# Weight halves by casting and accumulating loads, in place of a load, a cast and a subtraction

## The chip, the core and the metric

The kernel runs on one core of one Trainium2 chip. A core has five engines that run side by side and wait for each other by semaphores: TensorE (PE, matrix products; its weight loads are shown as PEld), VectorE (DVE), ScalarE (ACT), GpSimd (POOL) and SyncE (SP, which here only issues transfers). Transfers between the device memory and the on-chip memory run on 16 DMA engines; SyncE or GpSimd issue them. The metric is the time of one execution on the device, in microseconds, as the median of several runs.

## The reference, cut to what matters

One layer of a hybrid encoder is computed for 512 prompt tokens and 32 tokens of a running stream, 544 columns together: an input projection, three token mixers in parallel (RG-LRU, Mamba-2 SSD and HGRN2), their merge by gates, an output projection, and a SwiGLU FFN.

```python
h = rmsnorm(x, p['norm_mix'])
proj = h @ p['w_in']
z, xbc, dt_raw, hq, hf, hi, hgate, rgate, rx, mg = jnp.split(proj, split_pts, axis=-1)
...
pb = jnp.einsum('kblc,kcd->kbld', branches, p['w_branch'])
gates = jax.nn.sigmoid(mg.reshape(b, L, N_BRANCH, D_MODEL))
merged = jnp.einsum('kbld,blkd->bld', pb, gates)
x = x + merged @ p['w_out']
h2 = rmsnorm(x, p['norm_ffn'])
g, u = jnp.split(h2 @ p['w_ffn_in'], [FF_HIDDEN], axis=-1)
x = x + (jax.nn.silu(g) * u) @ p['w_ffn_out']
```

All of `w_in`, `w_branch`, `w_out`, `w_ffn_in` and `w_ffn_out` is float32, some 100 MB, and is read once.

## The kernel before

The products need more precision than one pass gives, so each operand is split into two halves of the type fp32r: a high half (the value cast to fp32r) and a low half (the value minus the high half). For weights w and activations x, TensorE adds up wh·xh + wh·xl + wl·xh.

All weights are cut into 101 groups of 256 columns, called **keys** here (lines 65 to 88). A key holds 8 blocks of 128 rows (128 x 2048 float32 on chip, 1 MB), but for the four last keys of `w_ffn_out`, which hold 6. Each key serves two **steps**: a step is one tile of 128 output columns, with 8 blocks times three passes times two halves of the tokens = 48 matmuls of 128x272. Within a step the products (line 263) run wh against both halves of the activations first, 32 matmuls, then wl against the high half, 16 matmuls.

How the weights come: `load_raw` (line 241) has SyncE load a key's float32 into `raw`, a pool with two buffers. `prep` (line 248) makes the halves of one step: ScalarE casts 128x1024 into `wh` (line 258), VectorE subtracts it from `raw` into `wl` (line 259); both pools have three buffers of a step's size. `run_program` (line 284) goes through the list of steps, has the halves prepared one step ahead, and the keys loaded two keys ahead of the preparation. What each engine does in which order is settled when the program is built; each engine then runs its list in order.

Between the products stands the mixers' work, in three stages: the RG-LRU (to about 190 us), the SSD (to about 490 us) and the HGRN2 (585 to 856 us). It uses VectorE, ScalarE, GpSimd and small matmuls. After each step an evacuation reads the step's accumulator (two buffers) by ScalarE or VectorE. From 493 to 585 us and after 856 us (branch product, output projection, FFN) TensorE has products alone.

GpSimd in the program before issues no transfers; it fills and copies small tiles, raises to the power -0.5 for the norms (line 167 and line 1064), and in the HGRN2 copies the blocks `bd` into `at` (line 1013).

The head (line 443) is written by hand: SyncE loads x (eight tiles `xt`) and in between the first key, rx0, in four pieces; ScalarE and VectorE split x (`yr`) and rx0 block by block; three tiles of products start before the norm of x is known, two from rx0 and one from the second key, rg0. The norm's factor `rs_x` comes from a sum of squares `ssx` (line 465), a power on GpSimd (line 167), and is brought into the layout of the columns by transposes on TensorE (line 172).

Of the kernel before, what the change touches and what calls it, by code (L numbers as in the profile page):

```python
# [11 lines left out]
F = _mybir.dt.float32  # L12
R = _mybir.dt.float32r
# [5 lines left out]
P = 128  # L19
# [18 lines left out]
LEVELS = (16, 32, 64)  # L38
# pacing of the mixers' work between the products: DVE microseconds to a tile of products, by phase
PACE_RG, PACE_RG_END, PACE_SSD, PACE_HG = 3.0, 4.0, 5.5, 3.5  # L40
# [13 lines left out]

# columns of the packed parameters, by channel of a tile; the first NHALF are used halved
HALVED = (("ba", 8), ("bi", 8))
# [8 lines left out]
def weight_groups():  # L65
    """key -> its blocks (matrix, first row, rows, first column, columns), 256 columns together"""
    g = {}
    for i in range(4):
        g[f"rx{i}"] = [("w_in", 0, D, C_RX + 256 * i, 256)]
        g[f"rg{i}"] = [("w_in", 0, D, C_RG + 256 * i, 256)]  # L70
        g[f"bc{i}"] = [("w_in", 0, D, C_XBC + 1024 + P * i, P), ("w_in", 0, D, C_XBC + 1536 + P * i, P)]
        g[f"xb{i}"] = [("w_in", 0, D, C_XBC + 256 * i, 256)]
        g[f"z{i}"] = [("w_in", 0, D, C_Z + 256 * i, 256)]
        for nm, c in (("hf", C_HF), ("hq", C_HQ), ("hi", C_HI), ("hgt", C_HG)):
            g[f"{nm}{i}"] = [("w_in", 0, D, c + 256 * i, 256)]
        for b in range(3):
            g[f"mg{b}_{i}"] = [("w_in", 0, D, C_MG + D * b + 256 * i, 256)]
            g[f"br{b}_{i}"] = [(f"w_branch{b}", 0, D, 256 * i, 256)]
        g[f"wo{i}"] = [("w_out", 0, D, 256 * i, 256)]
        for kg, (k0, nk) in enumerate(KG):  # L80
            g[f"fo{i}_{kg}"] = [("w_ffn_out", k0 * P, nk * P, 256 * i, 256)]
    for m in range(NF):
        g[f"fi{m}"] = [("w_ffn_in", 0, D, P * m, P), ("w_ffn_in", 0, D, FF + P * m, P)]
    return g
# [16 lines left out]
def hybrid_layer(ctx: ExitStack, tc: _tile.TileContext, a: dict, outs: list):  # L101
# [27 lines left out]

    # ---------------------------------------------------------------- constants and parameters  # L130
    hhi = hpool.tile([P, NK, T], R, tag="hhi", name="hhi")
# [26 lines left out]
    def token_rstd(ssq, n, name):  # L158
        """1/sqrt(mean + eps) by token, from squares summed over the channel tiles"""
        p = mx()  # L160
# [13 lines left out]

    # ---------------------------------------------------------------- derived parameters
    hga1, hgna1, hgb1, rgc, rgnc = (ctile([P, 8], n) for n in ("hga1", "hgna1", "hgb1", "rgc", "rgnc"))
# [24 lines left out]
    def derived():  # L201
        # a softmax over the layers, minus its first row summed up: one layer, so each row is its own maximum
        lbv = ctile([P, 8], "lbv")
# [13 lines left out]

    # ---------------------------------------------------------------- the stream of matrix products
    sides = []
# [18 lines left out]

    RAWB = 2

    def load_raw(key):
        g, nk = WG[key]
        t = wpool.tile([P, NK, 256], F, tag="raw", name="raw", bufs=RAWB)
        nc.sync.dma_start(t[:, :nk, :], wp[g].rearrange("p (k n) -> p k n", n=256)[:, :nk, :])
        raws[key] = t


    def prep(st):
        if st.wh is not None:
            return  # L250
        if st.share:
            st.wh, st.wl = st.share.wh, st.share.wl
            return
        r = raws[st.raw]
        st.wh = wpool.tile([P, NK, P], R, tag="wh", name="wh")
        st.wl = wpool.tile([P, NK, P], R, tag="wl", name="wl")
        src = r[:, : st.nk, st.col : st.col + P]
        S.activation(st.wh[:, : st.nk, :], src, AF.Copy)  # L258
        V.tensor_tensor(st.wl[:, : st.nk, :], src, st.wh[:, : st.nk, :].bitcast(F), ALU.subtract)  # L259

# [23 lines left out]
    def run_program():  # L284
# [9 lines left out]
        for s in program:  # L294
# [3 lines left out]
            while prepped < min(len(order), done + 2):  # L298
                st = order[prepped]
                while loaded < min(len(keys), pos[st.raw] + RAWB):  # L300
                    if keys[loaded] not in raws:
                        load_raw(keys[loaded])
                    loaded += 1
                prep(st)
                prepped += 1
# [12 lines left out]

    # phase pools ------------------------------------------------------------
    st_yr = ExitStack()  # L320
# [56 lines left out]

    # ---------------------------------------------------------------- gates and branches
    gate_th = {}
# [33 lines left out]

    # ---------------------------------------------------------------- RG-LRU
    sd = {}
# [19 lines left out]

    # ---------------------------------------------------------------- head
    # the first tiles take x before its norm, and the norm's factor by token after the products
    hd = {}
# [4 lines left out]
    def head():  # L443
# [8 lines left out]
        load_raw("rg0")  # L452
        whs = [wpool.tile([P, NK, P], R, tag="wh", name="wh") for _ in range(2)]
        wls = [wpool.tile([P, NK, P], R, tag="wl", name="wl") for _ in range(2)]
        derived()
# [162 lines left out]

    # ---------------------------------------------------------------- SSD
    xb_cv, gz, y_mb = {}, {}, {}  # L620
# [67 lines left out]
    def ssd_side(g):  # L688
# [29 lines left out]
        yield 3.0  # L718
        # C B^T and token-major B
        p = mx()  # L720
# [24 lines left out]
        dt, eacs, etot, wend = (sd[k] for k in ("dt", "eacs", "etot", "wend"))  # L745
        # token-major x, times dt and times the decay to the chunk's end
        xdt = pt_([P, 4, 256], "xdt")
# [21 lines left out]
        yield 0.7  # L769
        # states  # L770
        Hh = pt_([P, 4, 256], "Hh")
# [22 lines left out]

        # outputs
        yint = pt_([P, 4, 256], "xw")
# [19 lines left out]
        yield 0.6  # L816
        # both parts by channel, skip, gate, norm
        p5 = mx()
# [63 lines left out]

    # ---------------------------------------------------------------- HGRN
    hv, y_hg = {}, {}
# [34 lines left out]
    def hg_side(h):  # L919
# [21 lines left out]
        bds = pt_([TS, 32], "bds", 2)  # L941
        # within 16 tokens by two levels of four parts each: in every block, the queries of the parts
        # after part 0, 1 and 2, decayed to the part's end, meet its keys, also decayed to the part's end
        qv = pt_([P, T // 4, 10], "qv", 1)
# [148 lines left out]

    # ---------------------------------------------------------------- merge out, residual
    x1 = {}
# [26 lines left out]

    # ---------------------------------------------------------------- FFN
    ff = {}
# [64 lines left out]
    def fin_evac(m, hs):  # L1189
        """the tokens of some halves: the residual, token-major, times the norm's weight, and its squares"""  # L1190
        def f(acc):
# [64 lines left out]
def lay_out(v):  # L1256
    """The arrays that the program takes, from those of setup_inputs: layout only."""
    cm = lambda x: x.reshape(-1, P).T
# [64 lines left out]
```

## Time and profile before

| what | us |
|---|---|
| median of 3 runs | 1379.65 (1379.39 to 1381.41) |
| span of the profiled execution, first to last instruction | 1377.6 |
| outside the span, by the median | 2.05 |
| TensorE busy | 1359.3 |
| VectorE, ScalarE, GpSimd busy | 725.0, 531.3, 101.5 |
| bytes moved | 115.37 MB, mean 84 GB/s |

The profile has one such page and answers to queries on the trace behind it. A row of a group reads: line of the kernel, engine, operation, output from inputs with partitions x elements and type, number of such instructions, then the busy time and the mean time of one in nanoseconds, then how long the engine sat idle ahead of them and what ended that. A row of the timeline starts with the time from the span's start and the duration in us. A row of the windows lists, for a stretch of time, the busy time of each engine with its number of instructions, the granted clock of TensorE, the share of the 16 DMA engines in use, and the GB/s. In a row of waits stand the waiting engine with its line, the engine and line waited for, and the us in total, the times and the longest.

### The profile page before, as it was taken

To read this page: it belongs to the slowest core of one execution; us is meant where nothing else is said; L and a number is where in the kernel's file an instruction comes from. 1 tells how busy PE (TensorE), PEld (TensorE's weight loads), DVE (VectorE), ACT (ScalarE), POOL (GpSimd) and SP (SyncE) were. 2 spreads that over 40 slices of the span, in tenths; PEclk is the share of its full clock that TensorE was granted. 3 is DMA by queue.
4 is the path that set the end of the run, shared out by engine and by line. 5 is a ranking of instruction groups with operands and counts; after the bars stand their busy time and mean duration, and the time that the engine had idled before them with its cause. 6 is when DMAs were issued, how large, how long until landed. Compare 5 with 4: busy or idle time off the path is not lost.

```text
span 1377.6 us, 26147 instructions
## 1 busy us (share of the span) xinstructions
PE 1359.3 (99%) x11374; PEld 1316.6 (96%) x11374; DVE 725.0 (53%) x1337; ACT 531.3 (39%) x884; POOL 101.5 (7%) x200
## 2 busy tenths in 40 slices
PE   7999999999999999999999999999999999999997
PEld 7999999899998999999999999999999999999996
DVE  7987654737575644374747464455443443332222
ACT  6785744235445321333343433234222222222222
POOL 2031001021020000011010101000000000000000
PEclk9999999999999999999999999999999999999998
DMA  6212122212121122221212121242222222222211
GB/s 232 93 62 93 62 96 87 79 62 70 66 72 66 70 82 83 85 68 68 70 67 88 49 85 47 92 157 93 73 81 93 92 92 92 88 83 87 87 73 65
DMA packets 23634, 115.37 MB, mean 84 GB/s; under 512 B 2624, under 2 KB 7616, under 8 KB 11488
## 3 DMA queue, kind: packets, MB, share of 16 engines
q1 hardware_dynamic: 23520, 113.70, 23.6%
q8 instruction: 89, 1.46, 0.4%
q14 instruction: 25, 0.20, 0.0%
HBM read 109.29 MB, written 4.41 MB: 83 GB/s over the span
## 4 chain that ended last, share of the span: by engine, by line
PE 96%; DVE 1%; ACT 1%; issue 1%; DMA 0%; POOL 0%; SPq 0%; POOLq 0%; DVEq 0%
PE acc L277 83%; PE mx L563 1%; PE mx L829 1%; PE mx L831 1%; PE mx L972 1%; PE mx L1036 1%; PE mx L1051 1%; PE mx L931 1%; PE mx L776 1%; PE mx L1018 0%; PE mx L162 0%; PE mx L705 0%; PE mx L1053 0%; DMA xt<-in_xT_dram 0%; PE mx L805 0%
## 5 line engine op out<-in xcount | busy, mean ns | idle before, releaser
L258 ACT ACTIVATE wh<-raw 128x1024 fp32r<-128x1024 f32 (+1 forms) x194 | 203.7, 1051 | 452.6 <-PE acc L277 435.7
L259 DVE TENSOR_TENSOR wl<-raw,wh 128x1024 fp32r<-128x1024 f32 (+1 forms) x194 | 234.7, 1210 | 195.8 <-PE acc L277 174.7
L277 PE MATMUL acc<-hhi,wh 128*128 128x272 f32 x1472 | 316.5, 294 | 0.0
L277 PE MATMUL acc<-hlo,wh 128*128 128x272 f32 x1472 | 306.6, 289 | 0.0
L277 PEld LDWEIGHTS acc<-hhi,wh 128*128 128x128 f32 x1472 | 232.1, 188 | 6.1 <-issue 1.5
L277 PEld LDWEIGHTS acc<-hlo,wh 128*128 128x128 f32 x1472 | 231.2, 188 | 0.5
L277 PE MATMUL acc<-hhi,wl 128*128 128x272 f32 x1472 | 206.7, 290 | 0.0
L277 PEld LDWEIGHTS acc<-hhi,wl 128*128 128x128 f32 x1472 | 191.8, 188 | 2.9 <-issue 1.3
L277 PE MATMUL acc<-x1lo,wh 128*128 128x272 f32 x704 | 146.1, 288 | 0.0
L277 PE MATMUL acc<-x1hi,wh 128*128 128x272 f32 x704 | 145.8, 288 | 0.0
L277 PEld LDWEIGHTS acc<-x1hi,wh 128*128 128x128 f32 x704 | 110.9, 188 | 0.0
L277 PEld LDWEIGHTS acc<-x1lo,wh 128*128 128x128 f32 x704 | 110.4, 188 | 0.0
L277 PE MATMUL acc<-yr,wh 128*128 128x272 f32 x800 | 106.9, 289 | 0.1
L277 PEld LDWEIGHTS acc<-yr,wh 128*128 128x128 f32 x800 | 102.5, 188 | 0.9 <-ACT yr L345 0.3
L277 PE MATMUL acc<-x1hi,wl 128*128 128x272 f32 x704 | 96.0, 288 | 0.0
L277 PEld LDWEIGHTS acc<-x1hi,wl 128*128 128x128 f32 x704 | 91.4, 188 | 0.0
L277 PE MATMUL acc<-fhi,wh 128*128 128x272 f32 x352 | 74.7, 289 | 0.0
L277 PE MATMUL acc<-flo,wh 128*128 128x272 f32 x352 | 74.5, 289 | 0.0
L1158 DVE TENSOR_TENSOR fg<-acc,rb 128x544 f32<-128x544 f32 x22 | 15.9, 725 | 76.5 <-PE acc L277 74.6
L1169 DVE TENSOR_TENSOR fg<-fg,acc 128x544 f32<-128x544 f32 x22 | 15.9, 721 | 76.1 <-PE acc L277 76.1
L277 PEld LDWEIGHTS acc<-fhi,wh 128*128 128x128 f32 x352 | 55.8, 189 | 0.1
L277 PEld LDWEIGHTS acc<-flo,wh 128*128 128x128 f32 x352 | 55.8, 188 | 0.0
(368 smaller groups left out, 1748.9 us busy)
## 6 DMA issues: line engine op xcount, KB each, us to landing
raw<-in_weights_dram SPq DMA_DIRECT2D x93, 1024.0 KB, 4.7
raw<-in_weights_dram SPq DMA_DIRECT2D x4, 768.0 KB, 4.1
xt<-in_xT_dram SPq DMA_DIRECT2D x8, 272.0 KB, 5.7
yr<-in_xT_dram SPq DMA_DIRECT2D x8, 272.0 KB, 5.7
out_dram<-otok SPq DMA_DIRECT2D x4, 512.0 KB, 3.2
raw<-in_weights_dram SPq DMA_DIRECT2D x4, 256.0 KB, 5.6
wab<-in_rg_gates_dram SPq DMA_DIRECT2D x1, 1024.0 KB, 4.6
h0s<-in_ssm_in_dram SPq DMA_DIRECT2D x4, 128.0 KB, 3.9
```

The costliest lines, as they stand in the source:

```text
L258: S.activation(st.wh[:, : st.nk, :], src, AF.Copy)
L259: V.tensor_tensor(st.wl[:, : st.nk, :], src, st.wh[:, : st.nk, :].bitcast(F), ALU.subtract)
L277: PE.matmul(acc[:, h, :HALF], l, r[:, h * HALF : (h + 1) * HALF], start=st.first and i == 0, stop=st.last and i == len(seq) - 1)
L563: PE.matmul(p[:, :WH], l[:, i, ct, :], r[:, s], start=n == 0, stop=n == 2)
L776: PE.matmul(p[:, i * 256 : (i + 1) * 256], btok[:, c, :], xw[:, c, :], start=True, stop=True)
L829: PE.matmul(p[64 * (r % 2) : 64 * (r % 2) + 64, s], xdt[:, c, r * 64 : (r + 1) * 64], lts[c][:, r, :], start=c == 0, stop=False)
L831: PE.matmul(p[:, s], yint[:, c, j * P : (j + 1) * P], ident, start=False, stop=c == 3)
L931: PE.transpose(p[:, c * P : (c + 1) * P], src[:, c * P : (c + 1) * P], ident)
L972: PE.matmul(p[32 * b : 32 * b + 32, c * n : c * n + n], k[:, 32 * r : 32 * r + 32], vf[:, r * n : r * n + n], start=True, stop=True)
L1036: PE.matmul(p[:, c * P : (c + 1) * P], ktok[:, c, :], vtok[:, c, :], start=True, stop=True)
L1158: V.tensor_tensor(halves(t), acc[:, :, :HALF], halves(ff["rb"]), ALU.mult)
L1169: V.tensor_tensor(halves(t), halves(t), acc[:, :, :HALF], ALU.mult)
```

## The change

The float32 copy `raw` and the preparation by step go. Each key gets its two halves at once, in tiles of the key's size (128 x 8 x 256) with two buffers each:

```diff
-    RAWB = 2
+    RAWB = 1
     def load_raw(key):
         g, nk = WG[key]
-        t = wpool.tile([P, NK, 256], F, tag="raw", name="raw", bufs=RAWB)
-        nc.sync.dma_start(t[:, :nk, :], wp[g].rearrange("p (k n) -> p k n", n=256)[:, :nk, :])
-        raws[key] = t
+        src = wp[g].rearrange("p (k n) -> p k n", n=256)[:, :nk, :]
+        wh = wpool.tile([P, NK, 256], R, tag="wh", name="wh", bufs=2)
+        wl = wpool.tile([P, NK, 256], R, tag="wl", name="wl", bufs=2)
+        G.dma_start(wh[:, :nk, :], src)
+        S.activation(wl[:, :nk, :], wh[:, :nk, :].bitcast(F), AF.Copy, scale=-1.0)
+        G.dma_start(wl[:, :nk, :], src, accum_op=ALU.add)
+        raws[key] = wh, wl
     def prep(st):
-        if st.wh is not None:
-            return
-        if st.share:
-            st.wh, st.wl = st.share.wh, st.share.wl
-            return
-        r = raws[st.raw]
-        st.wh = wpool.tile([P, NK, P], R, tag="wh", name="wh")
-        st.wl = wpool.tile([P, NK, P], R, tag="wl", name="wl")
-        src = r[:, : st.nk, st.col : st.col + P]
-        S.activation(st.wh[:, : st.nk, :], src, AF.Copy)
-        V.tensor_tensor(st.wl[:, : st.nk, :], src, st.wh[:, : st.nk, :].bitcast(F), ALU.subtract)
+        wh, wl = raws[st.raw]
+        st.wh, st.wl = (t[:, :, st.col : st.col + P] for t in (wh, wl))
...
-                while loaded < min(len(keys), pos[st.raw] + RAWB):
+                while loaded < min(len(keys), pos[st.raw] + 2):
...
-        whs = [wpool.tile([P, NK, P], R, tag="wh", name="wh") for _ in range(2)]
-        wls = [wpool.tile([P, NK, P], R, tag="wl", name="wl") for _ in range(2)]
+        wh0, wl0 = (wpool.tile([P, NK, 256], R, tag=t, name=t, bufs=2) for t in ("wh", "wl"))
+        whs, wls = ([t[:, :, i * P : (i + 1) * P] for i in range(2)] for t in (wh0, wl0))
```

GpSimd issues a load that casts float32 into `wh`; ScalarE writes the negated high half into `wl`; GpSimd issues a second load of the same float32 that adds to what stands in `wl`. The key rx0 of the head keeps its way through `raw`, now a pool of one buffer. The sizes on chip stay the same: 16 + 24 KB a partition before, 8 + 32 KB now. In the changed kernel the lines after this place have numbers lower by 5: the load into `wh` is line 247, the negation line 248, the accumulating load line 249.

Three places of the engines' lists. First ScalarE's start of the program before, where `yr` is the cast of a tile of x and `wh` the cast of rx0:

```order
L469 ACTIVATE yr<-xt,pk 128x544
L190 ACTIVATE sp_lam<-sp_lam 128x8
L477 ACTIVATE wh<-raw 128x256 x2
L469 ACTIVATE yr<-xt,pk 128x544
L461 ACTIVATE ssx<-xt 128x544
```

The same place of the changed program:

```order
L464 ACTIVATE yr<-xt,pk 128x544
L190 ACTIVATE sp_lam<-sp_lam 128x8
L472 ACTIVATE wh<-raw 128x2x128 x2
L248 ACTIVATE wl<-wh 128x2048
L464 ACTIVATE yr<-xt,pk 128x544
L456 ACTIVATE ssx<-xt 128x544
```

The negation of rg0 has come in ahead of the second cast of x; the two casts of rg0 (line 258) stood behind all casts of x before. Second, ScalarE in the RG-LRU, at the end of the key rx1, before (`cv` are the evacuations, `gth` with `mx` is the tanh of the gates):

```order
L356 ACTIVATE cv<-acc 128x2x240
L258 ACTIVATE wh<-raw 128x1024
L363 ACTIVATE cv<-acc 128x2x32
L580 ACTIVATE gsq<-gsq 128x544
L552 ACTIVATE xrh<-xr 128x548
L586 ACT_TABLE_LOAD
L586 ACTIVATE gth<-gth 128x548
L258 ACTIVATE wh<-raw 128x1024
L564 ACT_TABLE_LOAD
L564 ACTIVATE gth<-mx_722,hpk 128x274
```

And now:

```order
L351 ACTIVATE cv<-acc 128x2x240
L547 ACTIVATE xrh<-xr 128x548
L358 ACTIVATE cv<-acc 128x2x32
L248 ACTIVATE wl<-wh 128x2048
L559 ACT_TABLE_LOAD
L559 ACTIVATE gth<-mx_712,hpk 128x274
```

One negation, which waits for the landing of `wh`, stands where the second of two casts stood, right ahead of the tanh. Third, GpSimd's list in the HGRN2 before, where `oss` is the norm's factor and `at` and `bd` are the mixer's blocks:

```order
L1013 COPY at<-bd 32x4x32 x4
L939 MEMSET at 128x512
L1064 TENSOR_TENSOR oss<-oss,mhalf 128x5
```

The same stage now:

```order
L247 DMA wh<-in_weights_dram 128x2048
L1008 COPY at<-bd 32x4x32 x4
L249 DMA wl<-in_weights_dram 128x2048
L934 MEMSET at 128x512
L1059 TENSOR_TENSOR oss<-oss,mhalf 128x5
L247 DMA wh<-in_weights_dram 128x2048
```

The loads have moved from SyncE's list into this one, and the copies, which wait for VectorE, stand between the load of a key's `wh` and that of its `wl`.

## The prediction

> **What bounds the kernel now.** I read the busy shares of the page first, then the chain that ended last.
>
> ```profile
> PE 1359.3 (99%) x11374; PEld 1316.6 (96%) x11374; DVE 725.0 (53%) x1337; ACT 531.3 (39%) x884; POOL 101.5 (7%) x200
> PE 96%; DVE 1%; ACT 1%; issue 1%; DMA 0%; POOL 0%; SPq 0%; POOLq 0%; DVEq 0%
> ```
>
> TensorE is busy for 99% of the span, and 96% of the chain is its own matmuls. No weight preparation and no transfer stands on the chain. So work taken from VectorE shortens nothing unless it stands in the few microseconds in which TensorE waits. The view of what TensorE waited for names nearly all of these, and both are in the head:
>
> ```profile
> PE acc L484 <- ACT wh L477: 6.3, 1, 6.3
> PE mx L172 <- POOL rs_x L167: 1.7, 1, 1.7
> ```
>
> What can be gained is thus some 2 us of the head (the 6.3 us are the first load and cast, which stay). What can be lost has no such limit: the question is whether the weights still come in time.
>
> **What goes.** From the costliest groups, with the landing times that the view of line 244 gives (least, median, longest):
>
> ```profile
> L258 ACT ACTIVATE wh<-raw 128x1024 fp32r<-128x1024 f32 (+1 forms) x194 | 203.7, 1051 | 452.6 <-PE acc L277 435.7
> L259 DVE TENSOR_TENSOR wl<-raw,wh 128x1024 fp32r<-128x1024 f32 (+1 forms) x194 | 234.7, 1210 | 195.8 <-PE acc L277 174.7
> raw<-in_weights_dram SPq DMA_DIRECT2D x93, 1024.0 KB, 4.7
> DMA to landing us min/median/max: 4.1/4.7/7.5
> q1 hardware_dynamic: 23520, 113.70, 23.6%
> ```
>
> VectorE loses 234.7 us. All of it lay beside products, so it is worth 0 here. ScalarE keeps its time: one negation of 128x2048 replaces two casts of 128x1024, 2 x 1.05 = 2.1 us to a key (a block of 256 weight columns, two steps of products). The transfers double in bytes read; at 23.6% of the engines now, the share would be about half, or 70% if the accumulating load counts twice. The sum of bytes is no bound either.
>
> **What comes: a chain in each key.** Before, SyncE's load of a key waited only for the casts that read the raw buffer, and ran a key ahead of them. Now a key's buffers are the ones TensorE reads, two of each: the load of key n+2 into wh waits until TensorE has read wh of key n for the last time; then the negation; then the accumulating load into wl. The time for this is read from the timeline of TensorE's weight loads in the FFN:
>
> ```profile
> 1004.10 2.08 PEld L277 LDWEIGHTS acc<-x1hi,wl 128*128 128x128 f32 x16
> 1006.12 0.32 PEld L277 LDWEIGHTS acc<-x1hi,wh 128*128 128x128 f32 x2
> 1010.15 2.08 PEld L277 LDWEIGHTS acc<-x1hi,wl 128*128 128x128 f32 x16
> 1012.16 0.32 PEld L277 LDWEIGHTS acc<-x1hi,wh 128*128 128x128 f32 x2
> ```
>
> A step starts with wh at 1006.12, turns to wl at 1010.15, 4.03 us later, and ends at 1012.16, 2.01 us after that: 6.04 us to a step, 12.08 to a key. Count from the end of key n. Its wh is free at -2.01, and wl of key n+2 is first read at 12.08 + 4.03 = 16.11. With D1 for the load into wh, 2.1 for the negation and D2 for the load into wl, -2.01 + D1 + 2.1 + D2 must not exceed 16.11: **D1 + D2 may be 16.0 us**. Every microsecond over it stops TensorE once in two keys (while it waits, the other pair of buffers gains the same time), so half a microsecond to a key. How many keys have only this to run on is counted from the rows of line 259 by stage (100 to 493, 493 to 585, 585 to 856, 856 to 1260 and 1260 to 1366 us):
>
> ```profile
> L259 DVE TENSOR_TENSOR wl<-raw,wh 128x1024 fp32r<-128x1024 f32 x53 | 64.7, 1221 | 67.4 <-PE acc L277 59.1 <-ACT wh L258 7.8 <-issue 0.3
> L259 DVE TENSOR_TENSOR wl<-raw,wh 128x1024 fp32r<-128x1024 f32 x16 | 19.6, 1223 | 30.8 <-PE acc L277 26.7 <-ACT wh L258 4.1
> L259 DVE TENSOR_TENSOR wl<-raw,wh 128x1024 fp32r<-128x1024 f32 x32 | 39.2, 1224 | 27.7 <-PE acc L277 26.7 <-issue 0.7
> L259 DVE TENSOR_TENSOR wl<-raw,wh 128x1024 fp32r<-128x1024 f32 (+1 forms) x67 | 81.1, 1211 | 27.2 <-PE acc L277 27.2
> L259 DVE TENSOR_TENSOR wl<-raw,wh 128x1024 fp32r<-128x1024 f32 (+1 forms) x17 | 19.2, 1129 | 51.8 <-PE acc L277 39.7 <-ACT wh L258 12.0
> ```
>
> Two rows are a key. Stages two, four and five hold products alone: (16 + 67 + 17) / 2 = 50 keys. In stages one and three the mixers' matmuls stand between: 393 us for 26.5 keys is 14.8 a key, 271 for 16 is 16.9, so the limit there is 2.7 or 4.8 us higher, at 18.7 and 20.8.
>
> **D1 and D2.** No load from GpSimd's queue, no casting and no accumulating load is in this trace. D1: the nearest row moves the same bytes to the same place, median 4.7 us, longest 7.5. I take 4.7. D2: the target is read as well as the source, so twice the bytes go in; it lies between 4.7 and 2 x 7.5 = 15.0, and I take twice the median, 9.4. The sum is 14.1, in a range from 9.4 to 22.5. So 1.9 us are left in each of the 50 keys, and the pure stretches cost **0**. On ScalarE the negation stands behind the copy of the step before (line 1165 of the changed kernel) and ahead of the next Silu; it would start at 2.7 and end at 4.8, before that Silu's input at about 7.
>
> Three keys have less: after a block of six (w_ffn_out's third) the key between lasts two steps of
>
> ```profile
> 1260.43 4.52 PE acc L277 x36
> ```
>
> so 9.04, not 12.08, and the limit is 13.0. Each waits 14.1 - 13.0 = 1.1: **+3.3**.
>
> **The head.** On ScalarE the negation of the first key now stands ahead of seven of the eight casts of x (the first pair of order rows).
>
> ```profile
> 0.00:8.00 8.00, 1.67 (x7) 1.68 (x8) 3.13 (x19) 3.93 (x9) 0.45 (x6) 1.00 0.75 219
> 8.00:16.00 8.00, 8.00 (x55) 8.00 (x54) 7.57 (x24) 8.00 (x18) 0.00 (x0) 1.00 0.99 380
> 7.33 0.75 ACT L469 ACTIVATE yr<-xt,pk 128x544 fp32r<-128x544 f32 x1 [0.75 <-DMA xt<-in_xT_dram]
> 9.28 0.33 SPq L244 DMA_DIRECT2D raw<-in_weights_dram  x1
> 18.35 1.04 ACT L258 ACTIVATE wh<-raw 128x1024 fp32r<-128x1024 f32 x1
> 20.79 1.21 DVE L259 TENSOR_TENSOR wl<-raw,wh 128x1024 fp32r<-128x1024 f32 x1
> 28.54 0.65 PE L172 MATMUL mx<-cst,rs_x 128*128 128x128 f32 x4 [1.72 <-POOL rs_x L167]
> ```
>
> The windows show the transfer share at 0.75 and 0.99 and, in the second, ScalarE busy for all 8.00 us. The first key's load was issued at 9.28, after x; now it goes out at about 1 us and shares the engines with x. If both get half of some 1.9 MB in 6 us, its 1 MB is there at about 8.5 to 9, the negation ends at about 11, and the second cast of x, at 7.33 before, starts 3.7 late. ScalarE has no gap after that to catch up in, apart from the 1.04 at 18.35; VectorE gives back the 1.21 at 20.79 that stood in the sum of squares. 3.7 - 1.0 is about **+3** at 28.54, between 0 (the load lands before 6.6) and 5 (it lands at 10).
>
> **The mixers.** The negation stands in ScalarE's queue and waits there for a landing; behind it is the tanh of the RG-LRU's gates, and TensorE waits for that. In the trace such a place is:
>
> ```profile
> 55.16 0.30 PEld L277 LDWEIGHTS acc<-hhi,wh 128*128 128x128 f32 x2
> 61.26 1.28 ACT L564 ACT_TABLE_LOAD   x1
> 62.55 1.74 ACT L564 ACTIVATE gth<-mx,hpk 128x274 f32<-128x274 f32 x4
> ```
>
> A key ends at 55.16 and the tanh starts 7.4 us later. Now: landing at -2.0 + 4.7 = 2.7, negation to 4.8, table to 6.1: in time. With D1 at 7.5 it is 8.9, 1.5 late, in some ten keys. So 0 to 15; I take a fifth, **+3**.
>
> The sum is 0 + 3.3 + 3 + 3 = +9.3 on the span of 1377.6, so 1386.9; the median of the runs, 1379.65, lies 2.05 above that span, which gives **1389**.
>
> **The rivals.**
>
> *The chain is longer than a key* (chance 0.32). It decides at D1 + D2 = 16.0, inside the range 9.4 to 22.5. At its middle, 18.5: 50 x 2.5 / 2 = 62, the three short keys 1.5 each more, head and mixers 10: about 1456. At 22.5: 50 x 6.5 / 2 = 162 and the mixers' keys as well, (26 x 3.8 + 16 x 1.7) / 2 = 63: about 1615. For it: two loads in series with an engine between them, and hops not counted. Against it: the transfer engines are three quarters idle.
>
> The Trainium skill speaks for this rival: "DMA: Bandwidth & Descriptors", section "Bandwidth", lists 6.15 us of engine time for 1 MB loaded by GpSimd's queue, and "Collectives: The Full Stack", section "Part 3: Why 7× under link rate — side-by-side accounting", says that an adding transfer runs at half the rate since it has two reads. By these pages, an estimate: D1 + D2 = 6.15 + 12.3 = 18.45, and 50 x 2.45 / 2 = 61 us of waits in place of none, about 1450. The 4.7 us from issue to landing on SyncE's queue speak against the first figure; for GpSimd's queue and for the second no run here shows anything.
>
> *GpSimd's queue couples the loads to the mixers* (0.15). In the HGRN stage the load into wl stands behind copies that wait for VectorE:
>
> ```profile
> L1013 POOL COPY at<-bd 32x128 f32<-32x128 f32 x32 | 17.5, 546 | 155.0 <-DVE bd L1008 154.0
> ```
>
> These copies waited 154.0 us in all. With 20.8 - 14.1 = 6.7 us to spare nothing happens until bd is 6.7 later than the negation; at 5 us beyond that for each of eight heads it is +40, about 1429.
>
> *Not slower* (0.17). The chain fits with room in all keys (D1 + D2 under 13.0) and the first load lands early, before 6.6 us: then the terms above are 0, and the time is the same, 1379.7. If besides the sum of squares, freed of the 1.21 us on VectorE, ends as much earlier and the wait of 1.72 at 28.54 goes, the kernel is 2.9 faster, 1376.7; it decides whether the first key is negated before ScalarE has a queue.
>
> **How the numbers follow.** The forecast has 0.36, the rivals 0.32, 0.15 and 0.17. Two tenths of a percent are 2.8 us, about what a measurement of this kernel can tell from no change. Of the 0.17, 0.05 is faster by more than that and 0.12 the same; the rest, 0.83, is slower. The range goes from 1378, which leaves out most of the faster case, to 1480, where D1 + D2 is 19.3 (50 x 3.3 / 2 = 83, with the other terms), which leaves out about 0.1 of the long chain.
>
> **What would show it.** Landing of line 247 about 5 us and of line 249 about 9 to 10. TensorE's waits for DMA into wl: three near 1274, 1308 and 1342 us of about 1 us, none from 860 to 1260. If the long chain is right, there is one in every second key there, all alike. The head: where the transposes of line 172 start, 31.5 against 28.54. If the queues are right, waits of TensorE stand between 585 and 856 and GpSimd's loads are issued late behind line 1008. The prediction is wrong if any of the stages of pure products grows by more than 1 us a key.

## The result, and the profile after

| | before | after |
|---|---|---|
| median of four runs, us | 1379.52 | 1460.59 |
| range of the runs | 1378.97 to 1381.41 | 1458.36 to 1465.52 |
| profiled execution, span | 1377.6 | 1456.6 |
| TensorE busy in it | 1359.3 | 1376.0 |

The changed kernel is slower: after over before is 1.0592, with a 95% interval from 1.0572 to 1.0612. The forecast was 1389, the range 1378 to 1480, and the rival "the chain is longer than a key" gave 1456.

From the page of the changed kernel, the busy shares, the software queue's share of the transfer engines' time, and the chain that ended last:

```profile
PE 1376.0 (94%) x11374; PEld 1323.8 (91%) x11374; DVE 512.5 (35%) x1143; ACT 511.5 (35%) x789; POOL 221.5 (15%) x394
q0 software_dynamic: 27936, 201.34, 56.6%
PE 51%; issue 31%; DMA 9%; POOL 4%; ACT 4%; DVE 1%; POOLq 0%; SPq 0%; DVEq 0%; ACTq 0%
```

VectorE is rid of 212.5 us of work (725.0 to 512.5; the prediction's 234.7 adds up single rows, and neighbouring rows overlap by some 0.1 us), and TensorE's own matmuls have gone from 96% of the chain to 51%. What TensorE waited for, in the whole execution (us in total, times, longest):

```profile
PE acc L272 <- DMA wl<-in_weights_dram: 39.1, 39, 5.2
PE acc L479 <- ACT wh L472: 9.5, 1, 9.5
PE mx L558 <- ACT gth L559: 8.0, 4, 3.0
PE mx L700 <- ACT lt L703: 3.9, 2, 2.8
PE acc L272 <- DVE merged L388: 2.9, 1, 2.9
PE acc L272 <- ACT hhi L518: 2.7, 1, 2.7
```

With seven smaller rows the waits add up to 71.1 us; before they were 8.8 (6.3, 1.7, 0.6 and 0.2). That is 62.3 of the 79.0 us by which the span grew. The other 16.7 are TensorE's busy time, 1376.0 against 1359.3: the same 11374 matmuls took longer. By place, the 62.3 are 39.1 in the stages of products alone (waits for the transfer into wl), 5.6 in the head (13.6 against 8.0), and 17.6 in the mixers (tanh, decays, merges).

How a key runs in the FFN now is seen in the timeline of GpSimd and of ScalarE (start, duration, and in brackets the idle time before it and what ended it):

```profile
1054.64 0.86 POOL L249 DMA_DIRECT2D wl<-in_weights_dram  x1 [10.88 <-ACT wl L248]
1056.54 0.55 POOL L247 DMA_DIRECT2D wh<-in_weights_dram  x1 [1.03 <-PE acc L272]
1065.14 1.92 ACT L248 ACTIVATE wl<-wh 128x2048 fp32r<-128x2048 f32 x1 [5.46 <-DMA wh<-in_weights_dram]
1067.36 0.86 POOL L249 DMA_DIRECT2D wl<-in_weights_dram  x1 [10.27 <-ACT wl L248]
```

From one adding load to the next are 12.72 us; a key of products has 12.08. This round is one of the shorter ones: the 21 rounds between the adding loads issued at 1015.84 and 1291.47 us, in the FFN's first product, take 12.6 to 14.8 us, 13.1 in the mean. What lengthens the longer ones was not followed up. The load into wh goes out at 1056.54, and the negation that waits for it starts at 1065.14: **8.6 us**, where the prediction had 4.7. The windows of the same stretch say where that time goes (last two columns: share of the transfer engines, GB/s):

```profile
1056.00:1062.00 6.00, 6.00 (x50) 6.00 (x49) 1.45 (x2) 0.66 (x1) 0.55 (x1) 1.00 0.97 180
1062.00:1065.00 3.00, 2.63 (x21) 2.41 (x20) 0.05 (x1) 0.00 (x0) 0.00 (x0) 1.00 0.87 344
1065.00:1068.00 3.00, 3.00 (x26) 3.00 (x25) 1.03 (x2) 2.46 (x2) 0.64 (x1) 1.00 0.00 0
```

For 6 us the engines are full at 180 GB/s: 1.08 MB, by the amount the adding load issued at 1054.64. Then 3 us at 344 GB/s: 1.03 MB, by the amount the load into wh, which was issued 5.5 us before that (at 1056.54). Then, while the negation runs, they do nothing. The two loads of neighbouring keys stand in one queue, one behind the other. Over the whole execution the times from issue to landing are (least, median, longest; the load into wh, line 247, then the adding load, line 249):

```profile
DMA to landing us min/median/max: 4.9/7.5/14.1
DMA to landing us min/median/max: 7.0/8.1/11.4
```

### The profile page after: what moved, and what is told of

Read it like the earlier page. It is cut to its first block, busy times and chain, and to the rows that moved or that the text cites. A ratio compares the mean times of both kernels' runs of the same rounds, so it can differ in the third digit from the quotient of the medians.

```text
span 1456.6 us, 25930 instructions
## 1 busy us (share of the span) xinstructions
PE 1376.0 (94%) x11374; PEld 1323.8 (91%) x11374; DVE 512.5 (35%) x1143; ACT 511.5 (35%) x789; POOL 221.5 (15%) x394
## 4 chain that ended last, share of the span: by engine, by line
PE 51%; issue 31%; DMA 9%; POOL 4%; ACT 4%; DVE 1%; POOLq 0%; SPq 0%; DVEq 0%; ACTq 0%
PE acc L272 41%; DMA wh<-in_weights_dram 5%; DMA wl<-in_weights_dram 3%; POOL wl L249 2%; ACT wl L248 1%; POOL wh L247 1%; PE mx L824 1%; PE mx L826 1%; PE mx L1031 1%; PE mx L967 1%; DMA raw<-in_weights_dram 1%; PE mx L1046 0%; PE mx L771 0%; DMA h0s<-in_ssm_in_dram 0%; PE mx L926 0%
## 5 line engine op out<-in xcount | busy, mean ns | idle before, releaser
L248 ACT ACTIVATE wl<-wh 128x2048 fp32r<-128x2048 f32 (+1 forms) x97 | 184.0, 1897 | 454.1 <-DMA wh<-in_weights_dram 413.6
L249 POOL DMA_DIRECT2D wl<-in_weights_dram x97 | 84.7, 874 | 753.7 <-ACT wl L248 630.2
L272 PE MATMUL acc<-x1hi,wl 128*128 128x272 f32 x704 | 97.6, 291 | 16.2 <-DMA wl<-in_weights_dram 16.2
L247 POOL DMA_DIRECT2D wh<-in_weights_dram x97 | 56.4, 581 | 274.4 <-PE acc L272 273.6
L272 PE MATMUL acc<-fhi,wl 128*128 128x272 f32 x352 | 49.4, 291 | 10.6 <-DMA wl<-in_weights_dram 10.6
L272 PEld LDWEIGHTS acc<-fhi,wl 128*128 128x128 f32 x352 | 45.6, 188 | 12.8 <-DMA wl<-in_weights_dram 12.8
```

Of the source, the lines that this page charges most:

```text
L247: G.dma_start(wh[:, :nk, :], src)
L248: S.activation(wl[:, :nk, :], wh[:, :nk, :].bitcast(F), AF.Copy, scale=-1.0)
L249: G.dma_start(wl[:, :nk, :], src, accum_op=ALU.add)
L272: PE.matmul(acc[:, h, :HALF], l, r[:, h * HALF : (h + 1) * HALF], start=st.first and i == 0, stop=st.last and i == len(seq) - 1)
```

## The experiments

Two theories stood after this. **The queue's order**: adding load of key n, then in the same queue the load into wh of key n+1, then the negation, then the adding load of key n+1; this round of one key takes 12.7 us and no buffer shortens it. **The buffers** (the prediction's sum): the load into wh can only start when TensorE releases one of two buffers, and from there to the use of wl there is not enough time.

**Without the addition.** The second load overwrites wl, so the kernel leaves the low half of the weights out.

```diff
-        G.dma_start(wl[:, :nk, :], src, accum_op=ALU.add)
+        G.dma_start(wl[:, :nk, :], src)
```

> The second load of each key overwrites wl with the rounded weights and adds nothing, so the low part of the weights is left out. Theory (the adding transfer is the price, and the next key's load into wh queues behind it): in the changed kernel 1 MB of the adding transfer keeps the engines busy for about 6 us (1068.0 to 1074.2) and 1 MB of the casting load for about 2.6; with two plain casting loads the round from one load into wl to the next shortens from 12.7 to about 12.7 - 3.5 = 9.2 us, under the 12.08 of a key, so the landing of the load into wl falls from 8.1 to about 5, that of the load into wh from 8.6 to about 5 to 6, no wait for wl is left from 860 us on, and the time is 1380 to 1395. Rival (any load from GpSimd's queue takes about 8 us, added or not): the landings stay at 7.5 to 8.6 and the time at 1450 to 1465.

Measured: 1391.05 us (one run). The issue to landing of the loads, into wh and into wl:

```profile
wh<-in_weights_dram POOLq DMA_DIRECT2D x93, 1024.0 KB, 5.0
wl<-in_weights_dram POOLq DMA_DIRECT2D x93, 1024.0 KB, 5.0
```

Both loads take 5.0, no wait for wl is left, and 69.5 of the 81 us are gone. A load from GpSimd's queue isn't slow; the addition is, and it makes the other load late. Both theories can live with this, since the prediction's sum also holds with 5.0 and 5.0.

**A third buffer for wh.** It takes the place of the buffer for raw.

```diff
-        wh = wpool.tile([P, NK, 256], R, tag="wh", name="wh", bufs=2)
+        wh = wpool.tile([P, NK, 256], R, tag="wh", name="wh", bufs=3)
...
-        raw = wpool.tile([P, NK, 256], F, tag="raw", name="raw", bufs=RAWB)
+        raw = wpool.tile([P, NK, 256], R, tag="wh", name="raw", bufs=3)[:, :, :].bitcast(F)
```

(wab's raw tile in the same way.)

> wh has three buffers in place of two (the third takes the place of raw), and all else is as in the changed kernel. Theory (one queue, in order): the load into wh of key n+1 is issued behind the adding load of key n and moves its bytes behind it, so the round of one key, adding load, casting load, negation, adding load, stays at 12.6 to 12.8 us whatever the buffers are, the waits for wl in the FFN stay, and the time is 1435 to 1460. Rival (the sum of the prediction: two buffers are too few, the load into wh starts too late): with a third buffer the load into wh has a whole key more, the FFN's period falls to 12.08, no wait for wl is left there, and the time is under 1415.

**The load into wh written a key ahead**, with the third buffer:

```diff
+                for k in keys[: pos[st.raw] + 3]:
+                    if k not in heads:
+                        load_head(k)
                 while loaded < min(len(keys), pos[st.raw] + 2):
```

(load_head allocates wh and issues its load; load_raw then only negates and adds.)

> As the run with three buffers for wh, but the load into wh of key n+2 is written ahead of the negation and the adding load of key n+1. Theory (one queue, in order): the casting load now moves ahead of the adding load, wh has landed a key before its negation, and only the adding load with 8 us is left between the release of wl and its use; the FFN's period is 12.08 without waits, the tanh of the RG-LRU's gates no longer waits behind a negation that waits for a landing, and the time is 1380 to 1392, what is left being the head. Rival (the engines' time: 8.5 us of transfers in 12.08 us of a key are too much, in whatever order): waits for wl stay, and the time is over 1420.

Measured: the third buffer alone 1387.7 us, ratio to before 1.0057 (1.0038 to 1.0076); with the load written ahead 1388.05, ratio 1.0062 (1.0047 to 1.0077). The first number is the one that the buffers had asked for, 72.9 us under the changed kernel, and against the queue's order as I had put it. But the two kernels give the same time for a reason: GpSimd's order is the same in both. With three buffers the scheduler itself put the load into wh of the next key ahead of the adding load. The order on GpSimd in the HGRN stage, in the changed kernel (a wh and the wl with the next number are one key):

```
L247 DMA wh_7188<-in_weights_dram 128x2048
L249 DMA wl_7189<-in_weights_dram 128x2048
...
L247 DMA wh_7396<-in_weights_dram 128x2048
...
L249 DMA wl_7397<-in_weights_dram 128x2048
```

and with three buffers:

```
L247 DMA wh_7396<-in_weights_dram 128x2048
L249 DMA wl_7189<-in_weights_dram 128x2048
...
L247 DMA wh_7590<-in_weights_dram 128x2048
L249 DMA wl_7397<-in_weights_dram 128x2048
```

The trace agrees over the whole execution: in the changed kernel GpSimd's loads into wh and wl alternate from the first to the last; with three buffers they begin wh, wl, wh, wh, wl and end with two loads into wl. So one edit had changed both the buffers and the order. The timeline of GpSimd with three buffers, in the FFN:

```profile
1043.70 0.55 POOL L247 DMA_DIRECT2D wh<-in_weights_dram  x1 [7.25 <-PE acc L272]
1047.67 0.87 POOL L249 DMA_DIRECT2D wl<-in_weights_dram  x1 [3.43 <-ACT wl L248]
1055.80 0.55 POOL L247 DMA_DIRECT2D wh<-in_weights_dram  x1 [7.25 <-PE acc L272]
1059.77 0.86 POOL L249 DMA_DIRECT2D wl<-in_weights_dram  x1 [3.42 <-ACT wl L248]
```

From adding load to adding load are 12.10 us, which is the products' own pace. The load into wh goes out 8.1 us behind an adding load, when that has about landed, and 4 us ahead of the next: it meets next to no other transfer (12 GB/s in the 2 us ahead of its bytes) and lands in 5.0 us (median; 7.5 in the changed kernel). Its landing times (least, median, longest), and the windows before and while its bytes move:

```profile
DMA to landing us min/median/max: 4.4/5.0/9.1
1043.00:1045.00 2.00, 2.00 (x18) 2.00 (x17) 0.00 (x0) 0.00 (x0) 0.55 (x1) 1.00 0.05 12
1045.00:1048.00 3.00, 3.00 (x26) 3.00 (x25) 0.77 (x2) 2.46 (x2) 0.33 (x1) 1.00 1.03 347
```

**The third buffer, with the order of the changed kernel.** This takes the two apart. The copy of one element reads wl of key n behind its negation, and all that writes the next wh comes behind it.

```diff
+            heads[after] = wpool.tile([P, NK, 256], R, tag="wh", name="wh", bufs=3)
+            G.tensor_copy(heads[after][:1, 0, :1], wl[:1, 0, :1].bitcast(F))
         G.dma_start(wl[:, :nk, :], src, accum_op=ALU.add)
...
+            G.dma_start(heads[after][:, :na, :], sa)
```

> Three buffers for wh, as in the run with three, but with the order of the changed kernel: GpSimd issues the load into wh of key n+1 directly behind the adding load of key n, which in the run with three buffers it issued the other way round (a copy of one element on GpSimd, from wl of key n into the next wh ahead of the adding load, holds it there). In the run with three buffers both the buffers and the order had changed. Theory (the queue's order): the load into wh stands 6 us behind the adding load, the negation of key n+1 waits for it, the adding load of key n+1 for the negation, and this round is 12.6 to 12.8 us against 12.08 of a key; the FFN has a wait for wl in every key, as in the changed kernel, the landing of the load into wh is 9 to 10 us, and the time is 1430 to 1465. Rival (the release of the buffers, as the prediction's sum had it): with the third buffer the FFN's period is 12.08, no wait for wl is left there, and the time is 1385 to 1400.

Measured: 1475.98 us, ratio to before 1.0691 (1.0675 to 1.0707). GpSimd's timeline, and the landing times of the load into wh and of the adding load (least, median, longest):

```profile
1072.41 0.86 POOL L263 DMA_DIRECT2D wl<-in_weights_dram  x1 [0.34 <-POOL wh L262]
1072.96 0.88 POOL L265 DMA_DIRECT2D wh<-in_weights_dram  x1
1085.50 0.86 POOL L263 DMA_DIRECT2D wl<-in_weights_dram  x1 [0.34 <-POOL wh L262]
```

```profile
DMA to landing us min/median/max: 6.0/10.2/14.2
DMA to landing us min/median/max: 6.8/8.1/12.2
```

With three buffers and this order all of the loss is back. The load into wh is issued at once, without waiting for a buffer, and lands after 10.2 us; the adding load ahead of it keeps its 8.1. The round shown is 13.09 us. The copy itself stands in it with 0.5 us (from its start at 1071.90 to 1072.41); the 12.6 that are left are still more than the 12.08 of a key. From 1005 to 1300 us TensorE waits 18.1 us for wl (16.2 in the changed kernel from 1006 to 1295). The time came out above the 1465 that I had expected: besides the copy there are three waits, of 11.8, 4.5 and 4.1 us, that the changed kernel does not have. The queue's order is the cause; the third buffer helps because it lets the order turn round. The fourth case, two buffers with the load into wh first, wasn't run: the adding load of a key would stand behind a load that waits for TensorE to finish the key before it.

**The negation on VectorE**, all else as in the changed kernel:

```diff
-        S.activation(wl[:, :nk, :], wh[:, :nk, :].bitcast(F), AF.Copy, scale=-1.0)
+        V.tensor_scalar(wl[:, :nk, :], wh[:, :nk, :].bitcast(F), -1.0, None, ALU.mult)
```

> The negation runs on VectorE, all else as in the changed kernel. Theory (in the mixers' stages the loss is ScalarE's queue standing behind a negation that waits for the landing of wh): TensorE's waits for gth, hhi and lt, 8.0 + 2.7 + 3.9 us in the changed kernel, go, or turn into waits for VectorE; the waits for wl in the FFN stay, since the round of the loads is the same; the time is 1430 to 1450. Rival (those waits come from late weights, on whichever engine): the time stays at 1455 to 1465 with waits of the same size before the same matmuls.

Measured: 1442.18 us (one run). The group of the negation, and the waits of TensorE:

```profile
L248 DVE TENSOR_SCALAR wl<-wh 128x2048 fp32r<-128x2048 f32 (+1 forms) x97 | 117.8, 1215 | 359.8 <-DMA wh<-in_weights_dram 354.5
```

```profile
PE acc L272 <- DMA wl<-in_weights_dram: 20.1, 18, 4.1
PE mx L1194 <- DVE x1f L1189: 7.2, 4, 3.3
PE mx L558 <- DVE xrl L548: 3.6, 3, 2.0
```

The waits for gth and lt are gone and others stand behind VectorE now (x1f, xrl): whichever engine waits for the landing of wh holds up its other work behind it. What I hadn't expected is the first of the waits: VectorE negates in 1.22 us, ScalarE in 1.90, and this 0.68 us out of the chain took the waits for wl from 39.1 to 20.1. Why only half went is seen in the rounds: the 21 between the adding loads at 1018.07 and 1288.16 us take 12.2 to 13.9 us, 12.9 in the mean, against 12.6 to 14.8 and 13.1 in the changed kernel. The shortest are 0.4 us shorter and still longer than the 12.08 of a key.

**What is left with three buffers** are 9 us over the kernel before. Its longer waits of TensorE are:

```profile
PE acc L479 <- ACT wh L472: 9.7, 1, 9.7
PE acc L272 <- DVE merged L388: 3.0, 1, 3.0
```

For the first (6.3 before) I made three runs. The first load of weights held back until the fifth tile of x has landed:

```diff
+        if key == "rg0":
+            G.tensor_copy(wh[:1, 0, :1], xt[:1, 4, :1])
         G.dma_start(wh[:, :nk, :], src)
```

> Three buffers for wh, and the first load of weights waits on GpSimd until the fifth tile of x has landed (about 10 us in place of 1.3; a copy of one element of x into wh ahead of it). Theory (the first load of 1 MB takes the engines from x and from the first weights): the wait of the first matmul falls from 9.7 to 6 to 7 us, the transposes of line 172 start 2 to 3 us earlier, and the time is 1383 to 1386, 2 to 4 under the run with three buffers; it is less if the later adding load makes the last of the head's products wait. Rival (the prediction's: the negation in ScalarE's queue sets the head's loss): the first matmul's wait stays at 9 to 10, and the time at 1386 to 1389.

The first key as before the change (SyncE behind x, casts, subtractions; its raw tile sits in a buffer of wh):

```diff
-        load_raw("rg0")
+        nc.sync.dma_start(raw0[:, :nk0, :], src0[:, :nk0, :])
...
+            S.activation(g0[:, :nk0, part], raw0[:, :nk0, part], AF.Copy)
+            V.tensor_tensor(l0[:, :nk0, part], raw0[:, :nk0, part], g0[:, :nk0, part].bitcast(F), ALU.subtract)
```

> Three buffers for wh, and the first key (rg0) is loaded and split as before the change: SyncE's queue behind x, casts on ScalarE, subtractions on VectorE; all other keys as in the run with three buffers. Theory (what is left of the loss there is in the head: the first casting load shares the engines with x and the first weights): the first matmul's wait falls from 9.7 to about 6.3, the median landing of the first weights (256 KB) from 7.8 to about 5.6, the transposes of line 172 start at 28 to 29, and the time is 1382 to 1385: of the 9 us over the kernel before, 3 to 5 go; the 3.0 us before the branch's products (VectorE waits there for a small load that shares the engines with the adding load) stay. Rival (the head's loss is ScalarE's order, whoever loads): the first matmul's wait stays over 9, and the time at 1386 to 1390.

The same with ScalarE's order in the head held to that of the kernel before:

```diff
-                    S.activation(whs[i][:, kh], src, AF.Copy)
+                    cast = S.activation(whs[i][:, kh], src, AF.Copy).ins
...
-            S.activation(hi, xt[:, k, :], AF.Identity, scale=pb("nm", k))
+            with tc.issue_after(cast) if k else ExitStack():
+                S.activation(hi, xt[:, k, :], AF.Identity, scale=pb("nm", k))
...
-                square(k - 1)
+                with tc.issue_after(cast):
+                    square(k - 1)
```

> As the run with rg0 loaded and split as before, but with ScalarE's order in the head held to that of the kernel before (each tile's cast of x and its square are issued behind the cast of the first weights ahead of them). In the run without this the first weights had landed as early as before (median 5.5 us), but ScalarE's order had them cast at 13.85 in place of 5.86 us, so it could not tell the head's cause. Theory (the first casting load shares the engines with x): the first matmul starts at 6.3 to 6.8 and the time is 1382 to 1385, 3 to 5 under the run with three buffers. Rival (what is left of the 9 us lies behind the head): the first matmul starts at 6.3 to 6.8, and the time is still 1386 to 1389.

Measured: 1395.18 (ratio 1.0107, 1.009 to 1.0124), 1393.51 (1.009, 1.0073 to 1.0107) and 1391.33 (1.0085, 1.0065 to 1.0104). None is faster than the 1387.7 of three buffers alone. The transfers did what was expected: the first weights (raw, 256 KB each) landed in 5.6 and 5.5 us in the first two, against 7.8. But in both the scheduler put ScalarE's casts of them behind several tiles of x, and the first matmul waited 10.8 and 14.3 us; in the first of the two TensorE waited another 5.2 us for the held-back load itself. With the order held it waited 5.7, and the gain was lost behind it:

```profile
PE acc L483 <- ACT wh L475: 5.7, 1, 5.7
PE acc L483 <- DVE wl L476: 2.9, 1, 2.9
PE acc L272 <- ACT hhi L528: 2.2, 1, 2.2
PE acc L272 <- DVE cv L360: 1.2, 1, 1.2
```

So the early load does make the first weights late, but this way of mending it costs as much elsewhere; my edit also takes a buffer of wh from the second and third key, so why isn't settled.

**The wait for merged.** In the run with three buffers VectorE stands for 6.1 us ahead of the merges, waiting for a load of 128 KB (h0s) that an SSD instruction, hns, needs:

```profile
194.86 0.43 DVE L784 TENSOR_TENSOR hns<-h0s,ex 128x256 f32<-128x256 f32 x1 [6.14 <-DMA h0s<-in_ssm_in_dram]
195.20 1.35 DVE L388 SCALAR_TENSOR_TENSOR merged<-merged,acc 128x544 f32<-128x544 f32 x2
```

That load landed 7.5 us after its issue; the same load in the kernel before took 3.8, and VectorE waited 2.48 for it, which cost nothing. The edit keeps hns behind the additions into Hh, where the program has it:

```diff
-                    V.tensor_tensor(Hh[:, c], Hh[:, c], d, ALU.add)
+                    last = V.tensor_tensor(Hh[:, c], Hh[:, c], d, ALU.add)
...
-        V.tensor_tensor(e3(hns), e3(h0s), bc(etot[:, 4, hs].unsqueeze(2), [P, 4, 64]), ALU.mult)
+        with tc.issue_after(last.ins):
+            V.tensor_tensor(e3(hns), e3(h0s), bc(etot[:, 4, hs].unsqueeze(2), [P, 4, 64]), ALU.mult)
```

On top of the kernel of the last run, and then on top of the one with three buffers alone:

> As the run before this one, and in the SSD VectorE issues the scaling of hns behind the last addition into Hh of its group, where the program has it, and not ahead of the branch's merges. Theory (VectorE waited 6.1 us there for the load of h0s, which shares the engines with the adding load and took 7.5 us in place of 3.8, and TensorE for the merge behind it): the wait of 3.0 us for merged goes and the time is 2 to 4 us under the run before this one, 1379 to 1383, the same as the kernel before the change within 0.3%. Rival (the products are late there for another reason): a wait of 2 to 4 us stays before the same products and the time does not change.

> The run with three buffers for wh (1387.7 us), with the one edit of the last run: VectorE scales hns behind the additions into Hh. The head is as in the changed kernel. If the wait of 3.0 us for merged is VectorE's wait for the load of h0s, it goes, and the time is 1383 to 1385; what is left over the kernel before, some 5 us, is the first load (9.7 against 6.3 us before the first matmul) and some 3 us by which TensorE's matmuls are longer (busy 1362.6 against 1359.3). If the wait only moves, the time stays at 1386 to 1389. None of the theories expects it under the kernel before.

Measured: 1387.05 us, 4.3 under the kernel that it is built on (ratio to before 1.0053, 1.0036 to 1.0069), and 1382.16 us, 5.5 under three buffers alone (ratio to before 1.0021, 1.0012 to 1.003). Both gained somewhat more than expected; the first did not come down to 1379 to 1383. In the second the waits of TensorE are:

```profile
PE acc L479 <- ACT wh L472: 10.0, 1, 10.0
PE mx L1195 <- DVE x1f L1190: 0.6, 1, 0.6
PE mx L558 <- ACT gth L559: 0.6, 1, 0.6
```

The wait for merged is gone, and TensorE's busy time fell with it from 1362.6 to 1360.1. This is the best version of the change: 78.4 of its 81 us are mended with one buffer and one instruction's place, and it is still 3 us slower than the kernel before (by the waits, 2.0 of them are the first load: 10.0 against 6.3, less the 1.7 before line 172 that is gone). Nothing that was tried beats the kernel before, which waits for 8.8 us in all.

## Why the prediction was wrong

**The sign, the bound and the range held.** No run shows a gain from the work taken from VectorE, and 1460.6 lies in the range. The forecast of +9.3 was wrong; +81 came. The sign that the prediction had set itself, more than 1 us a key in a stage of products alone, came too: the output projection grew from 48.4 to 58.9 us (2.6 for each of its 4 keys) and the FFN's second product from 137.0 to 150.8 (1.2 for each of 12); the FFN's first, from 268.1 to 289.1, has 0.95 for each of 22.

**The step that failed is D1 = 4.7.** I took it from the row of a load that SyncE issues a key ahead, alone in its queue. As the time of such a load it was right: 5.0 where nothing stands ahead of it. In the changed kernel it is 8.6 in the FFN, since each load into wh follows an adding load into the same queue by 1.9 us, and that one fills the engines for 6. I had written that two loads in series were a danger and that engines three quarters idle spoke against it; what counts is what stands in the queue at the moment of issue. D2 was 8.1, under the 9.4 that I took. With 8.6 and 8.1 the prediction's own sum is 16.7 against the limit of 16.0, and with two hand-overs that it left out (0.3 us each, from TensorE's last product with wh, which the profile's model ends at 1056.2, to GpSimd, and from the negation's end at 1067.06 to 1067.36) about 17.1, taking 1.92 for the negation: 0.55 us a key. The timeline has 12.72 - 12.08 = 0.64 in the round shown, and the mean round of 13.1 is 1.0 over. One reading of the profile before was wrong as well, without weight in the sum: SyncE's loads waited for VectorE's subtraction (line 259, 1101.3 us in 93 waits), and not for the casts.

**The mechanism was not the one that the sum describes.** It let the buffers set the end, with a wait in every second key. In the FFN's first product 20 of the 22 keys have one, in all 39 of the 50, and a third buffer with the old order cures nothing (1476): the round is one key long and runs through the queue. The rival of the long chain gave 1456 and was near, but by D1 + D2 = 18.5 and 62 us of waits; it was 16.7 and 39.1.

**The three short keys** (+3.3) can't be told apart from the others: from 1295 us on there are ten waits for wl, 10.6 us together.

**The head** (+3, at line 172). Those transposes start at 28.6 us, as before (28.54). The loss is before them, 9.5 against 6.3 at the first matmul, and after them (hhi 2.7, cv 1.2), 5.6 in all. The negation in ScalarE's queue, on which I had based it, is not what makes the first matmul late: the transfers are. The first weights land in 7.5 us (5.6 before), and ScalarE's first cast of them, which stands ahead of the negation, waits for them (before, then after):

```profile
5.86 0.72 ACT L477 ACTIVATE wh<-raw 128x256 fp32r<-128x256 f32 x2 [0.74 <-DMA raw<-in_weights_dram]
9.01 0.72 ACT L472 ACTIVATE wh<-raw 128x256 fp32r<-128x256 f32 x2 [4.27 <-DMA raw<-in_weights_dram]
```

I had seen that they share the engines, but let it delay only the negation. The delay that I had summed did come: the second cast of x starts at 11.44 in place of 7.33, though 3.2 us of that are the late first weights and none is a wait of the negation for its landing (it starts at 9.64, right behind the first casts); and the norm's sum is ready for the power on GpSimd some 2 us later than before. It cost nothing at line 172 because that power was shorter (before, then after):

```profile
25.03 3.46 POOL L167 TENSOR_TENSOR rs_x<-rs_x,mhalf 128x5 f32<-128x5 f32 x1 [5.45 <-DVE rs_x L166]
27.08 1.23 POOL L167 TENSOR_TENSOR rs_x<-rs_x,mhalf 128x5 f32<-128x5 f32 x1
```

In the kernel before, VectorE was busy with line 430 from 25.08 to 27.42 us beside the power; now it is idle from 26.72 to 28.97, while the power runs. Whether this is why was not tested.

**The mixers** (+3 out of 0 to 15). The mechanism was right: a negation that waits for its landing holds the tanh. It was mis-sized, with 17.6 us; the late D1 is in it, and a merge that waits for VectorE. With three buffers the wait for gth is 0.6 us.

**The matmuls' own time** was no term of the sum, and it grew by 16.7 us.

**GpSimd's queue coupled to the HGRN**: not borne out. From 624 to 882 us TensorE waited 1.2 us.

By the Trainium skill, "Collectives: The Full Stack", section "Part 3: Why 7× under link rate — side-by-side accounting", a collective's adding transfer runs at half the rate of a copy, and the trace agrees for this load: 180 against 344 GB/s. The 6.15 us of the Trainium skill's "DMA: Bandwidth & Descriptors", section "Bandwidth", for 1 MB from GpSimd's queue, are not borne out: the bytes of the load into wh took 3 us, at 344 GB/s. The same row of that table has 341 GB/s, which agrees; 1 MB in 6.15 us would be 170. That the two pages came near the result in the prediction was luck: both times that I worked out from them, 6.15 and 12.3, were too high (the bytes took 3 and 6 us), and the queue was in neither. The latter page of the Trainium skill has that as well: under "Two DMAs through the same engine are not ordered" it says that descriptors in one queue of an engine start in order. The landing times with the order held, 8.1 for the load in front and 10.2 for the one behind, agree.

## What to carry to other kernels

A transfer's time from another queue is its time when nothing stands ahead of it. Before it goes into a sum, write down what the same queue holds at the moment of issue, and close the loop: does this load wait behind one that itself waits for its successor's result? If a round is a few per cent longer than the work it feeds, every pass pays, however idle the engines are on average; an extra buffer helps only if it lets the issue order change, so look at the order that the scheduler made of it before calling the buffer the cause.

## What the hardware showed besides

**A pause slows the matmuls behind it.** In the output projection TensorE waits 5.2 us for wl, from 951.1 to 956.3; sixteen matmuls that take 2.16 us elsewhere then take 3.99. The windows show the granted clock (third number from the end) falling late in the wait and staying at about half until close to 962, some 5.5 us into the products:

```profile
956.30 3.99 PE L272 MATMUL acc<-mhi,wl 128*128 128x272 f32 x16 [5.20 <-DMA wl<-in_weights_dram]
```

```profile
954.00:956.00 2.00, 0.00 (x0) 0.00 (x0) 0.00 (x0) 0.00 (x0) 0.00 (x0) 0.74 1.00 299
956.00:958.00 2.00, 1.70 (x7) 1.70 (x8) 0.00 (x0) 0.00 (x0) 0.00 (x0) 0.50 0.99 390
958.00:960.00 2.00, 2.00 (x11) 2.00 (x10) 0.00 (x0) 0.49 (x1) 0.00 (x0) 0.50 0.08 23
960.00:962.00 2.00, 2.00 (x12) 2.00 (x11) 0.73 (x1) 2.00 (x3) 0.28 (x1) 0.55 0.00 0
962.00:964.00 2.00, 2.00 (x19) 2.00 (x18) 0.79 (x1) 0.61 (x2) 0.59 (x1) 1.00 0.56 53
```

The mean clock of the execution is 0.992 against 0.997, which by estimate is some 7 of the 16.7 us (0.5% of 1360). Short waits cost a little more than themselves too, without a lower clock: sixteen matmuls behind a wait of 0.37 us took 2.28 us in place of 2.16. How the rest divides wasn't tested.

**The adding load slows others too.** The 128 KB of h0s, on SyncE's queue, took 7.5 us in place of 3.8 in the run with three buffers. It was issued at 187.34, 1.1 us behind an adding load, and from 189 to 193 us the windows show the engines full (shares of 0.91 to 1.06) at 188 to 205 GB/s.
